# An encoder trunk on one core: transfers behind a power, one activation table for another, squares and gated units moved to later products

## The chip, the cores and the metric

The kernel runs on one core of a Trainium2 chip. The time is the device time of the program in microseconds (us), the median of several runs. The core has a matrix engine (TensorE, PE), a vector engine (VectorE, DVE), an activation engine (ScalarE, ACT), a general engine (GpSimd, POOL) and a queue engine (SyncE, SP) that issues DMAs. ScalarE and GpSimd can issue DMAs as well. Each engine works through its own queue in order; between the queues there are semaphores. TensorE writes its sums to PSUM, of which this kernel uses eight banks in two pools of four ("mm" and "aux").

## What is computed

Two groups of tokens (512 and 256, together T = 768 columns, all widths 1024) go through two layers with shared weights. Cut to what matters here:

```python
def swiglu(h, wg, wu, wd):
    return (jax.nn.silu(h @ wg) * (h @ wu)) @ wd

def even_layer(x, ...):
    x = x + 0.5 * swiglu(rmsnorm(x, f1_n), f1_g, f1_u, f1_d)
    x = x + mixer_ab(rmsnorm(x, mix_n), ...)
    x = x + 0.5 * swiglu(rmsnorm(x, f2_n), f2_g, f2_u, f2_d)
    return x

def odd_layer(x, ...):
    x = x + 0.5 * swiglu(rmsnorm(x, f1_n), f1_g, f1_u, f1_d)
    x = x + mixer_c(rmsnorm(x, mix_n), ...)
    x = x + 0.5 * swiglu(rmsnorm(x, f2_n), f2_g, f2_u, f2_d)
    return x
```

So there are four feed-forward blocks with 2816 hidden columns, and two mixers. Everything is fp32.

## The kernel before

**Precision.** Each fp32 operand is split into a high half (ScalarE rounds it, `whi` for weights, L163) and a low half (VectorE subtracts, `wlo`, L164; for activations L250 and L251). A product is three matmuls per block of 128 rows: high by high, low activation by high weight, high activation by low weight. The low half of the weight is thus needed by the third matmul of a product. The ring of split weights holds five (`NW = 5`).

**Tiling.** The 768 columns lie in two halves of 384, half 0 and half 1. The 2816 hidden columns are taken in 11 pairs of 256. For each pair, gate and up are computed by a Strassen-like scheme of seven products of 2x2 blocks. They are named after the activation operand: b11, b21, t2, t3, t1, b22, n4; each is done for gate and then for up, with 12 matmuls of 384 columns. b11 and b21 use half 0 alone, the others use sums and differences of the halves and of the weight's blocks. Weight sums come partly from DMA: `wsum` (L140) loads one block with SyncE and adds the other to it with an accumulating transfer from GpSimd (L144); other sums are made on VectorE (`sums`, L713).

**Norm.** The scale of the RMS norm is applied after the products. For a half of the columns, ScalarE squares the eight tiles of x and VectorE adds them (`norm_add`, L277); TensorE sums columns into PSUM (`norm_tok`), ScalarE scales (L294), GpSimd takes the power -0.5 (`power`, L314), TensorE turns the result across partitions (`norm_spread`, L198), and ScalarE copies it to `acc` (L455). A gated unit (`hidden`, L579) takes a gate and an up of one half: VectorE multiplies both by `acc` (L585, L587), ScalarE applies Silu (L586), VectorE multiplies them (L588). These feed the operands of the down product: `operands` makes them in eleven steps, six of them splits, five of them differences, and hands them out one at a time to whoever asks.

**Order.** The order of TensorE's instructions is the order in which the code traces them. The other engines' queues are ordered by a planner that follows the traced order where it can; `issue_after(i)` puts instructions of one engine behind instruction `i` in its queue. Two things set what is traced when. `self.after[p, b]` holds functions that run when the up weight of product b in pair p has been split. And `chains` are generators with due times in a clock `self.t` that only counts planned matmul time (1.92 for a product); `run_until` forces them when something needs their result, so that the norm's matmuls are traced there.

**The start.** In the first layer (`behind` is true there) pairs 0, 1 and 2 start with b11 and b21 while the inputs still arrive (`ORDER`, `stages`). Then pair 0 goes on with t2, t3, t1, b22, n4, then pair 1, then pair 2, and the down product of pairs 0 and 1 follows. When the up weight of pair 0's t1 is split, `after[0, "t1"]` runs: eight squares of half 1 and their additions (`squares`), which also starts half 1's norm chain with the delays 9.0 and 3.0, and the gated units of half 0 for pairs 1 and 2. At pair 0's n4, pair 1's transfers and weight sums follow. The gated units of half 1 for pair 0 wait until pair 1's t2 (`later`). The load of an activation table on ScalarE is inserted where an instruction needs a set that is not loaded; the first activation, `first` (L1729), is a Copy.

Of the kernel before, what the change touches and what calls it, by code (L numbers as in the profile page):

```python
# [33 lines left out]
DELAYS = (11.5, 3.0), (9.0, 3.0)  # L34
# [16 lines left out]
class Trunk:  # L51
# [4 lines left out]
    def __init__(self, ctx, tc, aps, phases=PHASES):  # L56
# [8 lines left out]
        self.late = self.mark = self.turn = None  # L65
# [72 lines left out]
    def wsum(self, name, x, y):  # L138

        t = self.fw.tile([P, 4, P], F32, tag="s", name=name, bufs=8)  # L140
        f = t.rearrange("p a b -> p (a b)")
        with self.tc.issue_after(self.late) if self.late else nullcontext():
            self.nc.sync.dma_start(f, x)
        self.nc.gpsimd.dma_start(f, y, accum_op=ALU.add)  # L144
        return t
# [165 lines left out]
    def power(self, y, v):  # L311

        with self.tc.issue_after(self.turn) if self.turn else nullcontext():
            self.nc.gpsimd.tensor_tensor(out=y, in0=v, in1=self.minus[:, : y.shape[1]], op=ALU.pow)  # L314
# [143 lines left out]
    def ffn(self, pre):  # L458
# [50 lines left out]
        def pair(p):  # L509
# [56 lines left out]

            def keep(out, key, n):

                e[n, out] = etile(out)
                nc.scalar.copy(e[n, out], bank[key, n])  # L570
                if p != 1 or out != "u2":
                    next(steps, None)

            def add(key, n, other):
                t = e[n, other]
                nc.vector.tensor_tensor(out=t, in0=bank[key, n], in1=t, op=ALU.add)  # L576
                next(steps, None)
# [17 lines left out]
            def later(f):  # L595
                if p:
                    f()
                else:
                    self.after.setdefault((1, "t2"), []).append(f)
# [39 lines left out]
            def p4():  # L639
                for n in names:  # L640
                    product(n, a[n, 2, 2], "n4", "Y", False)
                    next(steps, None)
                hidden(1, 0, bank["Y", "gate"], bank["Y", "up"])

            def p3():
# [3 lines left out]
                later(lambda: hidden(0, 1, e["gate", "u2"], e["up", "u2"]))  # L649

            if early:
# [6 lines left out]
                yield  # L658
                hidden(0, 0, bank["X", "gate"], bank["X", "up"])
# [7 lines left out]
            if p:  # L667
                load_all()
                if p < EARLY:
                    with self.tc.issue_after(self.behind[1]):  # L670
                        for n in names:
                            sums(n, "s2")
# [13 lines left out]
        units = [lambda: next(stages[1]), lambda: next(stages[2])]  # L686
        if behind:
            self.after[0, "t1"] = [self.squares] + units
        else:
            self.after[0, "t3"] = units  # L690
        self.after[0, "n4"] = [lambda: next(stages[1])]
# [1013 lines left out]
    def build(self):  # L1705
# [20 lines left out]
        elif kind != "last":  # L1726
# [3 lines left out]
            self.np_.tile([P, 6], F32, tag="sm", name="first", bufs=3), self.minus, AF.Copy, scale=1.0  # L1730
# [157 lines left out]
```

## Time and profile before

| | us |
|---|---|
| median of 3 runs | 2585.97 |
| lowest, highest | 2585.16, 2588.82 |
| the profiled run | 2585.71 |
| its span | 2583.9 |

The profile is of one execution. Its page gives busy time by engine; the stage tables give the same for a stretch of time. The waits name the engine and line that waited, what released it, and total, number and longest. A timeline lists start, duration, engine, line, operation and tiles (out<-in), and in square brackets the idle time ahead of an instruction and what ended it. Neighbours of the same kind are merged into one row with their number. Tile names follow the code without buffer numbers; b220h is the high half of block 0 of operand b22.

### The profile page before, as it was taken

Reading aid. Unit: us, or ns where it says so; the run is one execution under the profiler, and the core shown is the slowest. Engines: PE = TensorE matmul, PEld = TensorE weight load, DVE = VectorE, ACT = ScalarE, POOL = GpSimd, SP = SyncE. Lnnn points to the kernel's source line nnn. Section 1 sums busy time; section 2 is a strip of 40 time slices with the busy share of each in tenths; the row PEclk is TensorE's granted clock in tenths of the full one; section 3 lists DMA queues with packets and bytes.
Section 4 is the critical chain, followed back from the end, with each engine's and each line's share of the span. In section 5 each row is a group of like instructions: output and inputs, shape, how many; then the busy total and the mean of one; then the engine's idle time right before and its main releaser. Section 6 shows DMA issues by size and latency. Waiting matters only on the chain.

```text
span 2583.9 us, 42568 instructions
## 1 busy us (share of the span) xinstructions
PE 2557.8 (99%) x15160; PEld 2499.0 (97%) x15160; DVE 2099.9 (81%) x4206; ACT 1370.6 (53%) x2845; POOL 323.3 (13%) x398
## 2 busy tenths in 40 slices
PE   8999999999999999999999999999999999999998
PEld 7999999988899999999999999998999999999998
DVE  8888788879879778788988878886767598878887
ACT  6544454646756545445654445564555475444553
POOL 1111111000111111110111111102212111101100
PEclk9999999999999999999999999999999999999999
DMA  7655556342146545453565455432222256545451
GB/s 205 167 132 126 122 134 159 113 122 68 58 139 158 144 120 130 123 129 88 144 155 135 115 126 127 123 117 77 62 62 65 87 146 168 129 118 124 122 124 51
DMA packets 187156, 310.88 MB, mean 120 GB/s; under 512 B 31680, under 2 KB 46528, under 8 KB 186944
## 3 DMA queue, kind: packets, MB, share of 16 engines
q1 hardware_dynamic: 149792, 240.75, 29.8%
q0 software_dynamic: 36864, 67.13, 16.7%
q8 instruction: 119, 1.95, 0.3%
q14 instruction: 93, 0.76, 0.1%
q10 hardware_dynamic: 288, 0.29, 0.0%
HBM read 298.65 MB, written 15.07 MB: 121 GB/s over the span
## 4 chain that ended last, share of the span: by engine, by line
PE 93%; DVE 3%; ACT 1%; issue 1%; DMA 1%; POOL 0%; ACTq 0%; DVEq 0%; SPq 0%; POOLq 0%
PE ps_mm L187 61%; PE ps_aux L187 31%; PE ps_aux L198 1%; DVE wlo L164 1%; DMA x<-in_x 0%; DVE ol L251 0%; DMA raw<-in_w 0%; DVE s L713 0%; DVE tmp L397 0%; DVE u L576 0%; ACT xh L960 0%; ACT whi L163 0%; POOL sm L314 0%; ACT p L1157 0%; ACT oh L250 0%
## 5 line engine op out<-in xcount | busy, mean ns | idle before, releaser
L163 ACT CAST whi<-s 128x512 fp32r<-128x512 f32 x508 | 310.6, 620 | 404.1 <-PE ps_mm L187 212.7
L164 DVE TENSOR_TENSOR wlo<-s,whi 128x512 fp32r<-128x512 f32 x508 | 344.7, 688 | 180.3 <-ACT whi L163 163.5
L144 POOL DMA_DIRECT2D s<-in_w x256 | 223.6, 914 | 1468.2 <-DVE wlo L164 407.6
L163 ACT CAST whi<-rawp 128x512 fp32r<-128x512 f32 x344 | 211.5, 620 | 265.4 <-PE ps_mm L187 103.1
L164 DVE TENSOR_TENSOR wlo<-rawp,whi 128x512 fp32r<-128x512 f32 x344 | 235.1, 687 | 24.9 <-ACT whi L163 16.6
L187 PE MATMUL ps_mm<-db,whi 128*128 128x384 f32 (+1 forms) x948 | 242.8, 337 | 0.0
L187 PE MATMUL ps_aux<-dt,whi 128*128 128x384 f32 x880 | 225.7, 337 | 0.0
L187 PEld LDWEIGHTS ps_mm<-db,whi 128*128 128x128 f32 x948 | 171.9, 188 | 0.0
L187 PE MATMUL ps_mm<-db,wlo 128*128 128x384 f32 (+1 forms) x474 | 160.0, 337 | 0.6 <-DVE wlo L164 0.6
L187 PEld LDWEIGHTS ps_aux<-dt,whi 128*128 128x128 f32 x880 | 159.8, 188 | 0.0
L187 PE MATMUL ps_aux<-dt,wlo 128*128 128x384 f32 x440 | 148.4, 337 | 0.0
L187 PE MATMUL ps_mm<-xh,whi 128*128 128x512 f32 (+1 forms) x416 | 144.2, 347 | 0.0
L163 ACT CAST whi<-raw 128x512 fp32r<-128x512 f32 x164 | 100.5, 620 | 80.3 <-PE ps_mm L187 55.8
L187 PE MATMUL ps_mm<-xh,wlo 128*128 128x512 f32 (+1 forms) x416 | 140.0, 337 | 0.0
L187 PE MATMUL ps_mm<-xl,whi 128*128 128x512 f32 (+1 forms) x416 | 140.0, 337 | 0.0
L164 DVE TENSOR_TENSOR wlo<-raw,whi 128x512 fp32r<-128x512 f32 x146 | 99.1, 688 | 27.7 <-ACT whi L163 26.5
L576 DVE TENSOR_TENSOR u<-ps_aux,u 128x384 f32<-128x384 f32 x176 | 97.4, 553 | 10.4 <-PE ps_aux L187 8.4
L1157 ACT ACTIVATE p<-p,st 128x256 f32<-128x256 f32 (+3 forms) x144 | 69.0, 481 | 53.4 <-DVE st L1152 53.4
L187 PEld LDWEIGHTS ps_mm<-db,wlo 128*128 128x128 f32 x474 | 88.9, 188 | 1.4 <-DVE wlo L164 1.4
L187 PEld LDWEIGHTS ps_mm<-xh,whi 128*128 128x128 f32 x416 | 78.2, 188 | 10.0 <-issue 1.3
L187 PEld LDWEIGHTS ps_mm<-xh,wlo 128*128 128x128 f32 x416 | 78.1, 188 | 9.4
L187 PEld LDWEIGHTS ps_mm<-xl,whi 128*128 128x128 f32 x416 | 78.3, 188 | 7.5
(508 smaller groups left out, 8059.3 us busy)
## 6 DMA issues: line engine op xcount, KB each, us to landing
rawp<-in_w SPq DMA_DIRECT2D x384, 256.0 KB, 3.2
s<-in_w SPq DMA_DIRECT2D x256, 256.0 KB, 2.9
s<-in_w POOLq DMA_DIRECT2D x256, 256.0 KB, 4.8
raw<-in_w SPq DMA_DIRECT2D x163, 256.0 KB, 2.9
xdm<-x SPq DMA_DIRECT2D x16, 384.0 KB, 2.4
x<-in_x SPq DMA_DIRECT2D x16, 192.0 KB, 4.7
x<-xdm SPq DMA_DIRECT2D x8, 384.0 KB, 3.8
tab<-skew SPq DMA_DIRECT2D x8, 256.0 KB, 4.6
```

Of the source, the lines that this page charges most:

```text
L144: self.nc.gpsimd.dma_start(f, y, accum_op=ALU.add)
L163: i = nc.scalar.copy(hi, src).ins
L164: self.behind = i, (eng or nc.gpsimd).tensor_tensor(out=lo, in0=src, in1=hi.bitcast(F32), op=ALU.subtract).ins
L187: self.nc.tensor.matmul(out, lhsT=lhsT, rhs=rhs, start=start, stop=stop, **kw)
L198: self.nc.tensor.transpose(out, src, self.ident)
L576: nc.vector.tensor_tensor(out=t, in0=bank[key, n], in1=t, op=ALU.add)
L1157: nc.scalar.activation(outs[i - n0], outs[i - n0], AF.Exp, scale=-1.0, bias=mn[:, i : i + 1], accum_out=sm[:, i : i + 1])
```

## The change

It has three parts.

1. In `wsum`, the accumulating transfers of the loads that are marked late (`self.late`: pair 0's sums) are queued on GpSimd behind the last traced power. `power` notes its instruction for this.
2. The first activation of the program uses Silu instead of Copy, so that the table loaded at the start is Silu's.
3. In the first layer, the squares of half 1 run at pair 1's t3, the gated unit of pair 1 at pair 0's n4 (behind pair 1's loads and weight sums), and that of pair 2 at pair 1's t1. Pair 0's units of half 1 run at pair 1's b22 in the first layer and at its t3 in the other three feed-forwards, instead of t2. The delays of half 1's norm become 6.0 and 1.8. The steps of pair 0's operands, which pair 1 asks for, are spread otherwise: in the first layer none at t3, t1 and b22, three at each n4 product and the rest at the end of the pair; in the others two at each addition (t1, b22) and two at each n4.

```diff
-DELAYS = (11.5, 3.0), (9.0, 3.0)
+DELAYS = (11.5, 3.0), (6.0, 1.8)
...
-        self.nc.gpsimd.dma_start(f, y, accum_op=ALU.add)
+        with self.tc.issue_after(self.powered) if self.late and self.powered else nullcontext():
+            self.nc.gpsimd.dma_start(f, y, accum_op=ALU.add)
...
         with self.tc.issue_after(self.turn) if self.turn else nullcontext():
-            self.nc.gpsimd.tensor_tensor(out=y, in0=v, in1=self.minus[:, : y.shape[1]], op=ALU.pow)
+            self.powered = self.nc.gpsimd.tensor_tensor(out=y, in0=v, in1=self.minus[:, : y.shape[1]], op=ALU.pow).ins
...
+            def ahead(n=2):
+                for _ in range(n if p == 1 else 1):
+                    next(steps, None)
+
             def keep(out, key, n):
...
-                if p != 1 or out != "u2":
+                if p != 1:
                     next(steps, None)
 
             def add(key, n, other):
...
-                next(steps, None)
+                ahead(0 if behind else 2)
...
-                    self.after.setdefault((1, "t2"), []).append(f)
+                    self.after.setdefault((1, "b22" if behind else "t3"), []).append(f)
...
                     product(n, a[n, 2, 2], "n4", "Y", False)
-                    next(steps, None)
+                    ahead(3 if behind else 2)
...
+            def second():
+                load_all()
+                if p < EARLY:
+                    with self.tc.issue_after(self.behind[1]):
+                        for n in names:
+                            sums(n, "s2")
...
                 p2()
                 yield
+                if behind and p == 1:
+                    second()
+                    yield
                 hidden(0, 0, bank["X", "gate"], bank["X", "up"])
                 yield
...
             if p:
-                load_all()
-                if p < EARLY:
-                    with self.tc.issue_after(self.behind[1]):
-                        for n in names:
-                            sums(n, "s2")
+                if not (behind and p == 1):
+                    second()
...
         units = [lambda: next(stages[1]), lambda: next(stages[2])]
+        ahead = lambda: next(stages[1])
         if behind:
-            self.after[0, "t1"] = [self.squares] + units
+            self.after[0, "n4"] = [ahead, units[0]]
+            self.after[1, "t3"] = [self.squares]
+            self.after[1, "t1"] = [units[1]]
         else:
             self.after[0, "t3"] = units
-        self.after[0, "n4"] = [lambda: next(stages[1])]
+            self.after[0, "n4"] = [ahead]
...
-            self.np_.tile([P, 6], F32, tag="sm", name="first", bufs=3), self.minus, AF.Copy, scale=1.0
+            self.np_.tile([P, 6], F32, tag="sm", name="first", bufs=3), self.minus, AF.Silu, scale=1.0
```

## Rows read from the trace of the kernel before

**Rows 1.** The page's first part: busy time, share of the span, instructions by engine.
```profile
PE 2557.8 (99%) x15160; PEld 2499.0 (97%) x15160; DVE 2099.9 (81%) x4206; ACT 1370.6 (53%) x2845; POOL 323.3 (13%) x398
```

**Rows 2.** TensorE's waits over the span: for whom, total us, times, longest.
```profile
PE ps_aux L198 <- POOL sm L314: 6.2, 3, 3.3
...
PE ps_mm L187 <- DVE wlo L164: 3.3, 4, 1.3
```

**Rows 3.** Timeline of TensorE, 20 to 31 us: start, duration, instruction, idle ahead.
```profile
20.15 0.80 PE L187 MATMUL ps_aux<-ones,acc 128*128 128x1 f32 x6 [0.17 <-DVE acc L277]
...
26.48 0.59 PE L198 MATMUL ps_aux<-ident,sm 128*128 128x128 f32 x3 [3.30 <-POOL sm L314]
26.78 0.62 PE L187 MATMUL ps_mm<-b211h,whi 128*128 128x384 f32 x1
...
30.07 0.42 PE L187 MATMUL ps_aux<-b110l,whi 128*128 128x384 f32 x1
```

**Rows 4.** Timeline of TensorE, 57 to 91 us.
```profile
57.35 0.69 PE L187 MATMUL ps_aux<-b220h,wlo 128*128 128x384 f32 x1 [5.54 <-DVE wlo L164]
...
60.72 0.46 PE L187 MATMUL ps_aux<-b220h,whi 128*128 128x384 f32 x1
...
62.95 0.72 PE L187 MATMUL ps_aux<-ones,acc 128*128 128x1 f32 x6
...
65.11 0.54 PE L198 MATMUL ps_aux<-ident,sm 128*128 128x128 f32 x3 [0.80 <-POOL sm L314]
...
90.66 0.34 PE L187 MATMUL ps_mm<-t20h,wlo 128*128 128x384 f32 x1
```

**Rows 5.** Stage table: stretch, length, TensorE busy, granted clock, DMA share, GB/s.
```profile
57.30:60.80 3.50, 3.45 (x11) 0.50 0.00 0
```

**Rows 6.** Stage table of VectorE: stretch, length, busy, clock, DMA share, GB/s.
```profile
25.67:89.33 63.66, 56.79 (x110) 0.92 0.60 139
```

**Rows 7.** Timeline of VectorE, 25 to 93 us.
```profile
28.03 0.56 DVE L251 TENSOR_TENSOR t21l<-tmp,t21h 128x384 fp32r<-128x384 f32 x1 [2.36 <-ACT t21h L250]
...
34.64 0.56 DVE L588 SCALAR_TENSOR_TENSOR sg<-sg,v 128x384 f32<-128x384 f32 x1 [2.12 <-ACT sg L586]
...
66.20 0.56 DVE L585 TENSOR_TENSOR u<-u,acc 128x384 f32<-128x384 f32 x1 [1.08 <-ACT acc L455]
...
88.87 0.55 DVE L588 SCALAR_TENSOR_TENSOR u<-u,u 128x384 f32<-128x384 f32 x1
89.33 1.29 DVE L164 TENSOR_TENSOR wlo<-s,whi 128x512 fp32r<-128x512 f32 x2
...
92.07 0.55 DVE L251 TENSOR_TENSOR db<-u,db 128x384 fp32r<-128x384 f32 x1
```

**Rows 8.** Timeline of ScalarE, 22 to 33 us.
```profile
22.07 0.15 ACT L294 ACTIVATE sm<-ps_aux 128x3 f32<-128x3 f32 x1
...
27.11 0.48 ACT L455 COPY acc<-ps_aux 128x384 f32<-128x384 f32 x1 [2.99 <-PE ps_aux L198]
...
32.79 1.28 ACT L586 ACT_TABLE_LOAD   x1
```

**Rows 9.** Timeline of GpSimd, 0 to 130 us.
```profile
21.59 3.74 POOL L144 DMA_DIRECT2D s<-in_w  x4 [18.15 <-DMA s<-in_w]
24.16 2.27 POOL L314 TENSOR_TENSOR sm<-sm,minus 128x3 f32<-128x3 f32 x1
...
63.97 1.09 POOL L314 TENSOR_TENSOR sm<-sm,minus 128x3 f32<-128x3 f32 x1 [19.84 <-ACT sm L294]
```

**Rows 10.** DMA issues of GpSimd at 21.59 and at 24.5: number, size, us to landing.
```profile
s<-in_w POOLq DMA_DIRECT2D x1, 256.0 KB, 5.5
...
s<-in_w POOLq DMA_DIRECT2D x1, 256.0 KB, 10.1
```

**Rows 11.** VectorE's groups by line, 44 to 56 us: busy, mean ns, idle before.
```profile
L277 DVE TENSOR_TENSOR acc<-acc,sq 128x384 f32<-128x384 f32 x7 | 3.8, 546 | 0.0
```

**Rows 12.** Timeline of TensorE, second feed-forward of layer 0.
```profile
808.20 0.45 PE L187 MATMUL ps_mm<-t30h,wlo 128*128 128x384 f32 x1 [1.34 <-DVE wlo L164]
```

More of the change, by code (lines that the diff above doesn't have):

```diff
@@ L64, in __init__ @@
         self.fed_last, self.after = {}, {}
-        self.late = self.mark = self.turn = None
+        self.late = self.mark = self.turn = self.powered = None
         self.first = []
```

## Prediction

> **What bounds the kernel now.** The page's first part comes first: TensorE is busy 99% of the span, so only its idle time and its slow time can be won [rows 1]. The view of its waits then names the idle time: 6.2 us for the power on GpSimd (three times, the longest 3.3) and 3.3 us in four waits for low halves (wlo) of weights [rows 2], beside a longer one shown below. The TensorE timeline puts the large ones into the first layer. One is 3.30 us long and ends at 26.48, where the turned norm of half 0 waits for the power [rows 3]; one is 5.54 us and ends at 57.35, where pair 0's b22 waits for its low half; one is 0.80 us, at 65.11, for half 1's power [rows 4]. After both long waits the matmuls follow each other at about 0.32 us instead of 0.176: from 26.78 to 30.07 ten steps take 3.29 us, 1.53 more than at full rate [rows 3], and from 57.35 to 60.72 eleven take 3.37, 1.44 more [rows 4]; the granted clock there is 0.50, the lower of its two levels, 1.2 of 2.4 GHz [rows 5]. The 0.80 us wait left the matmuls at 0.18. So on TensorE alone 3.30 + 1.53 + 5.54 + 1.44 + 0.80 = 12.6 us lie open.
>
> The second bound shows in the stage table for VectorE: between 25.67 and 89.33 it is busy 56.79 of 63.66 us, idle 6.87 [rows 6]. It ends with the low half for the first product (t2, gate) of pair 2, done at about 90.0 [rows 7] and used by TensorE at 90.66 [rows 4]. All of pairs 0 and 1 stands ahead of it in that queue, so moving work about inside the stretch cannot bring this product forward by more than VectorE's idle time.
>
> **Part by part.**
>
> *Accumulating transfers behind the power.* In the trace the four issues start at 21.59 and hold GpSimd 3.74 us; the power, whose input ScalarE finishes at 22.22 [rows 8], comes behind them and ends at 26.43 [rows 9]. Ahead of them it would start at about 22.3 and take 1.09 us, as the later one does [rows 9], so the turn runs at about 23.45: the wait falls from 3.30 to 0.3, a gain of 3.0, and the 1.5 us of slow matmuls behind it go too. The bounds of the power's own time are 1.09 and the 2.27 us of the first row [rows 9]; I take 1.09, because the longer one overlaps the end of the fourth issue; with 2.27 the gain is 1.9. ScalarE's copy of the scale at 27.11 [rows 8] then comes near 24.2, and VectorE's wait of 2.36 us before 28.03 [rows 7] disappears, since VectorE is busy until 25.67 anyway.
>
> The Trainium skill (GPSIMD Engine Reference, section Specifications) says that GpSimd shares its SBUF interfaces with VectorE and contends with VectorE instructions that read two SBUF inputs, which is what VectorE runs at that moment; by it the power would lie nearer the long end, and the sum above nearer 1.9 than 3.0. The later row of 1.09 us also ran beside such instructions, which speaks against much of it.
>
> The cost is on the transfers: issued 1.86 us later (23.45 instead of 21.59). In the trace the first landed 5.5 us after its issue and the fourth 10.1 after [rows 10], which is 27.1 and about 33.7; moved, the last lands between 33.7 (if the other transfers set the pace) and 35.6. It holds the up weight of t3. VectorE arrives there about 4 us earlier than now, near 34, so its in-order queue can stand 0 to 2 us; I take 0.9. By the Trainium skill (DMA: Bandwidth & Descriptors, section Anatomy of one DMA) a transfer of this size from GpSimd takes about 2.6 us from issue; then nothing would stand here, and the time would be 0.9 lower. The rows of 5.5 and 10.1 disagree with it.
>
> *Silu's table at the beginning.* The load at 32.79 takes 1.28 us [rows 8] and with Silu behind it keeps VectorE waiting 2.12 us before 34.64 [rows 7]. The load at the start exists already (for Copy); it changes its set and not its time. The wait falls to 0 to 0.3. TensorE does not wait there, so this is worth only what VectorE's queue is worth.
>
> *Squares and gated units.* Seven additions of squares (3.8 us busy [rows 11]) and the gated units of pairs 1 and 2 (six VectorE instructions at 0.55, 3.3 us) leave the place ahead of b22's low half: up to 7.1 us for a wait of 5.54, which goes, with the 1.4 us of slow matmuls. Pair 1's unit moves to pair 0's n4 and frees the PSUM banks from which pair 1's t2 starts; three VectorE instructions and a copy into the bank must then fit into n4's second product of 2.1 us; TensorE may wait 0 to 0.9. The squares go behind pair 1's t3, and the gated unit of pair 2 to its t1.
>
> The norm of half 1 moves with the squares. Its delay is 6.0 in the planner's time, while only three products of 1.92 lie between its start and the end of pair 1's t1, where the first gated unit of half 1 asks for the scale. So column sums and turn stand next to each other there, with nothing between. In the trace the sums run from 62.95 for 0.72 and the turn starts at 65.11 [rows 4]; the next matmul could have started near 63.53, so the wait is about 1.6 us where 0.8 stood. VectorE waited 1.08 for the same chain [rows 7], and I leave it 1.0.
>
> On TensorE alone: 12.6 - 0.3 (rest of the first wait) - 1.6 (new wait) = 10.7 us, so pair 2's t2 would be used at 80.0.
>
> On VectorE: of 6.87 us idle, 0.9 (landing), 1.0 (norm chain) and 0.3 (the small ones) remain, so 4.7 go. The slack of 90.66 against 90.0 stays usable for about 0.5: 5.2. Then the order: nine of the eleven steps that split pair 0's units for the down product stand ahead of 89.33 now, and the ninth and eleventh come behind (the first at 92.07 [rows 7]). The change traces six of them at pair 1's n4 and five at its end. If the five again fall behind pair 2's first weights, three steps leave the stretch, each 0.46 in the queue (the distance between the starts at 88.87 and 89.33 [rows 7]): +1.4. That makes 6.6, of which I give 0.2 away for small waits at pair 1's t2. **VectorE sets the gain of the first layer: 6.4 us**, not TensorE's 10.7. What is late next is pair 2's t2.
>
> *The other layers.* Pair 0's second-half units move from pair 1's t2 to its t3. In the second feed-forward of layer 0 TensorE waits 1.34 us before 808.20 for t3's low half [rows 12], which in the code stands behind the six VectorE instructions of those two units; the last feed-forward has its like, since four such waits make 3.3 us and none is over 1.3 [rows 2]. The wait goes, but the steps move as well (two behind each addition), and VectorE is nearly full there too: between 0 and 1.34 each, I take 0.7, together 1.4. The third one has no wait there. Their accumulating transfers already follow the power: 0.
>
> **Sum**: 6.4 + 1.4 = 7.8 us. The profiled run took 2585.71 (span 2583.9, 1.8 around it), 0.26 below the median of 2585.97, against which the time is given: **2578.2 us**.
>
> **Rivals.**
>
> *TensorE's own bound.* If the steps run behind pair 2's first weights (nine at 0.46 are 4.1 us of VectorE work) and the transfers cost nothing (0.9), the queue no longer sets the end: 10.7 + 2.6 = 13.3, 2572.7. For it: the last two steps do slip today. Against: the six at n4 are traced ahead of n4's second weight.
>
> *Strict order.* All eleven steps run before pair 2's weights: 5.2 - 0.9 = 4.3. TensorE then waits over 5 us in one place at pair 2's t2, and the slow matmuls return there (1.5): 2.8, with 0.7 from the other layers 3.5: 2582.5. For it: the squares' additions did stand ahead of b22's low half just as they were traced.
>
> *The power is not earlier*, because something else holds it: VectorE keeps its 2.36 us wait, 2580.6.
>
> *Slower: VectorE stands behind half 1's chain.* The gated units of pair 1 wait for the scale in the middle of VectorE's queue, with the weights of b22 and n4 behind them. Then about 18.4 us of VectorE work remain before pair 2's t2: five gated units of three instructions, eleven steps and four additions at 0.46 (13.8), five low halves and two weight sums at 0.65, half of the pair at 89.33 [rows 7] (4.6). The chain of half 0 took 7.4 us (sums at 20.15 [rows 3], the scale copied at 27.59 [rows 8]); if half 1's takes as long from the end of pair 1's t1 at about 69.5 (the 80.0 above, less four products of 2.1 and 2.2 for the chain itself), with nothing done meanwhile, the weight is ready at 95.3 and used 4.6 later than now; with 1.5 us of slow matmuls and no gain elsewhere, 2592.1. It decides where VectorE starts on that work after 70.8. Against: half 1's chain took 3.2 us in the trace (62.95 to VectorE's next start at 66.20 [rows 4, 7]), and the code lets VectorE run five weights ahead of TensorE.
>
> **How the numbers follow.** Forecast 0.48, TensorE's bound 0.15, strict order 0.25, power not earlier 0.05, slower 0.07. The forecast's own spread is 2575 to 2581 (landing 0 to 2, steps 0 to 1.4, other layers 0 to 2.6). The range reaches to TensorE's bound and past strict order: 2572.5 to 2584. About 0.2% (5.2 us) is what can be told from no change; 2580.8 is the line. Faster: 0.45 of the forecast, 0.15, 0.04 from strict order and 0.03 from the fourth case, 0.67. Slower 0.07. Within: 0.26.
>
> **What would show it.** The power ahead of the four transfers, and TensorE's wait there below 0.5; no table load near 33; no wait at pair 0's b22; sums and turn side by side at the end of pair 1's t1 with 1 to 2 us of wait; VectorE nearly without idle time until pair 2's t2, and TensorE's remaining waits there; no wait at t3 in the second and last feed-forward. It is wrong if VectorE has time to spare while TensorE waits, or if pair 2's t2 starts before 81.

## The result, and the profile after

The changed kernel takes 2591.15 us (median; 2589.22 to 2594.14) where the kernel before takes 2585.97. The ratio is 1.0017 (95% interval 1.0009 to 1.0025): slower by 0.17%, just inside what was called no difference, 13 us above the forecast of 2578.2 and above its range. One of the nine runs of e2 below, the profiled one, took 5630.37 us, so e2's median is that of the other eight and it has no trace to compare.

| | before | after |
|---|---|---|
| median, us | 2585.97 | 2591.15 |
| span of the profiled execution, us | 2583.9 | 2589.3 |
| TensorE busy, us | 2557.8 | 2562.6 |
| VectorE busy, us | 2099.9 | 2099.6 |
| ScalarE instructions | 2845 | 2844 |

The page's first part, for [rows 1]:

```profile
PE 2562.6 (99%) x15160; PEld 2499.3 (97%) x15160; DVE 2099.6 (81%) x4206; ACT 1370.9 (53%) x2844; POOL 325.4 (13%) x398
```

The work is the same but for one table load. TensorE is "busy" 4.8 us longer with as many instructions: part of its time is slower time. Its waits, for [rows 2] (for whom, total us, times, longest):

```profile
PE ps_mm L188 <- DVE wlo L165: 6.7, 9, 2.7
PE ps_aux L199 <- POOL sm L315: 3.5, 3, 1.8
PE ps_aux L188 <- DVE u L581: 3.1, 3, 1.4
PE ps_mm L188 <- ACT whi L164: 2.2, 4, 1.5
```

The power costs 2.7 us less than before. But low halves now cost 6.7 us in nine waits, high halves 2.2, and the third row is new: TensorE waits for VectorE's additions (L581) to free PSUM banks.

**The first stage did what was forecast.** GpSimd, for [rows 9]:

```profile
21.91 0.92 POOL L315 TENSOR_TENSOR sm<-sm,minus 128x3 f32<-128x3 f32 x1 [17.91 <-ACT sm L295]
22.78 3.74 POOL L145 DMA_DIRECT2D s<-in_w  x4
...
69.82 1.09 POOL L315 TENSOR_TENSOR sm<-sm,minus 128x3 f32<-128x3 f32 x1 [2.26 <-ACT sm L295]
```

The power is ahead of the four issues, and TensorE's timeline, for [rows 3] and [rows 4], has no wait at the turn of half 0 and none at pair 0's b22:

```profile
22.88 0.54 PE L199 MATMUL ps_aux<-ident,sm 128*128 128x128 f32 x3
...
70.97 0.54 PE L199 MATMUL ps_aux<-ident,sm 128*128 128x128 f32 x3 [1.44 <-POOL sm L315]
...
81.41 0.44 PE L188 MATMUL ps_mm<-t20h,whi 128*128 128x384 f32 x1 [1.46 <-ACT whi L164]
...
84.77 0.69 PE L188 MATMUL ps_mm<-t20h,wlo 128*128 128x384 f32 x1 [2.74 <-DVE wlo L165]
...
88.14 0.52 PE L188 MATMUL ps_mm<-t20h,whi 128*128 128x384 f32 x1
```

The last rows are pair 2's t2: TensorE was ready for it at 79.95, as worked out (80.0), and used the low half at 84.77, 5.9 us earlier than before. Then ten steps of matmuls take 84.77 to 88.14, 0.34 us each instead of 0.176. The stage table (stretch, length, busy of PE, PEld, DVE, ACT, POOL, clock, DMA share, GB/s):

```profile
84.00:91.00 7.00, 6.23 (x20) 6.23 (x21) 5.86 (x12) 3.60 (x9) 1.83 (x2) 0.51 0.80 180
```

The granted clock there is 0.51, the lower of the two levels. VectorE, for [rows 7]:

```profile
34.17 0.69 DVE L165 TENSOR_TENSOR wlo<-s,whi 128x512 fp32r<-128x512 f32 x1 [0.37 <-ACT whi L164]
...
72.06 0.56 DVE L590 TENSOR_TENSOR u<-u,acc 128x384 f32<-128x384 f32 x1 [1.90 <-ACT acc L456]
...
84.03 0.69 DVE L165 TENSOR_TENSOR wlo<-s,whi 128x512 fp32r<-128x512 f32 x1
```

Between 35 and 84 it stands still once, 1.90 us for half 1's scale; eight of the eleven operand steps stand ahead of the low half at 84.03.

**The later feed-forwards lost.** The same matmul in two traces shows where. The table gives the start of a low-half matmul against the kernel before, in us, at eight places: pair 1's b22 and pair 2's t2 and t3 of the first layer (before: 82.2, 90.7, 94.9), pair 3 of the same feed-forward, behind the first down product (149.6), then t3 in the second feed-forward (808.2), pair 1's b22 in the third (1306.8), pair 3 in the third (1390.7), and the first down product of the fourth, behind its pair 2 (2177.8). Each row is from one execution. The experiments, which the next sections tell, stand below it.

| kernel | 82.2 | 90.7 | 94.9 | 149.6 | 808.2 | 1306.8 | 1390.7 | 2177.8 |
|---|---|---|---|---|---|---|---|---|
| after | -10.5 | -5.9 | -3.0 | -2.7 | -4.2 | -0.1 | +3.7 | +5.2 |
| e3 first layer only | -9.4 | -3.9 | -1.3 | -1.6 | -1.5 | -1.5 | -1.5 | -1.1 |
| e4 power and table only | -3.2 | -3.2 | -3.2 | -2.8 | -2.7 | -2.8 | -2.8 | -2.7 |
| e8 squares and units only | -7.1 | -1.4 | +0.2 | +0.6 | +0.5 | +0.5 | +0.5 | +0.5 |
| e6 steps behind t2 | -9.5 | -8.5 | -8.3 | -1.4 | -1.6 | -1.8 | -1.8 | -1.8 |
| e7 matmuls in the wait | -10.0 | -5.3 | -4.7 | -4.4 | -4.3 | -4.4 | -4.4 | -4.2 |
| e9 last five held | -9.9 | -4.8 | -3.6 | -3.7 | -3.7 | -3.9 | -3.9 | -4.1 |
| e10 squares at t2 | -9.4 | -3.3 | -3.2 | -2.9 | -3.1 | -3.1 | -3.1 | -2.9 |
| e11 t3's low half first | -9.5 | -4.3 | -3.7 | -3.6 | -5.3 | -4.1 | -4.1 | -4.2 |
| e12 less vector work | -9.9 | -4.2 | -4.1 | +1.9 | +0.4 | +3.0 | +3.0 | +1.4 |
| e1 one step per addition | -9.3 | -4.7 | -1.9 | -1.9 | -3.2 | -1.7 | +0.4 | +0.5 |
| e5 steps from t3 | -9.5 | -4.9 | -2.4 | -2.6 | -4.2 | -2.8 | -1.1 | -1.0 |
| e13 changed, with matmuls | -9.4 | -4.8 | -4.2 | -3.9 | -5.4 | -1.9 | +2.5 | +5.2 |

Row "after": 2.7 us are won in the first layer; of 10.5 at pair 1's b22, 4.6 go until pair 2's t2 and 2.9 at the low clock behind it. The t3 wait of [rows 12] is gone (-2.7 to -4.2), but from 149.6 us on the later feed-forwards, with what they win at t3 counted in, lose 2.6, 3.8 and 1.5 (columns 149.6, 1306.8, 1390.7, 2177.8), 7.9 in all: -2.7 + 7.9 = +5.2. In the third one, VectorE's queue in the changed kernel reads:

```profile
1302.83 0.69 DVE L165 TENSOR_TENSOR wlo<-rawp,whi 128x512 fp32r<-128x512 f32 x1 [1.40 <-ACT whi L164]
1303.62 0.56 DVE L252 TENSOR_TENSOR db<-sg,db 128x384 fp32r<-128x384 f32 x1
...
1312.64 0.55 DVE L593 SCALAR_TENSOR_TENSOR u<-u,u 128x384 f32<-128x384 f32 x1
1313.11 0.69 DVE L165 TENSOR_TENSOR wlo<-rawp,whi 128x512 fp32r<-128x512 f32 x1
```

The two low halves are those of n4's gate and up. Between them stand ten operand steps and ten additions and gated-unit instructions, from 1303.62 to 1313.11 with no idle time. TensorE:

```profile
1313.85 0.45 PE L188 MATMUL ps_mm<-n40h,wlo 128*128 128x384 f32 x1 [0.76 <-DVE wlo L165]
...
1330.94 0.44 PE L188 MATMUL ps_aux<-b220h,whi 128*128 128x384 f32 x1 [1.42 <-DVE u L581]
```

The second wait comes from late transfers. GpSimd issued the accumulating transfers for that stretch at 1318.27 and 1319.95, where the kernel before had issued both from 1315.67 on (its row stands second):

```profile
1318.27 0.86 POOL L145 DMA_DIRECT2D s<-in_w  x1 [18.33 <-DVE s L728]
```

```profile
1315.67 1.76 POOL L144 DMA_DIRECT2D s<-in_w  x2 [15.70 <-DVE v L587]
```

VectorE then stood for the sum that the first one brings, ahead of the additions that free the banks; before, it did not (again second):

```profile
1324.97 0.69 DVE L728 TENSOR_TENSOR s<-s,rawp 128x512 f32<-128x512 f32 x1 [1.69 <-issue]
```

```profile
1323.17 0.68 DVE L713 TENSOR_TENSOR s<-s,rawp 128x512 f32<-128x512 f32 x1
```

### The profile page after: what moved, and what is told of

The parts are those of the page before. It is cut to its first block, busy times and chain, and to the rows that moved or that the text cites. A ratio compares the mean times of both kernels' runs of the same rounds, so it can differ in the third digit from the quotient of the medians.

```text
span 2589.3 us, 42560 instructions
## 1 busy us (share of the span) xinstructions
PE 2562.6 (99%) x15160; PEld 2499.3 (97%) x15160; DVE 2099.6 (81%) x4206; ACT 1370.9 (53%) x2844; POOL 325.4 (13%) x398
## 4 chain that ended last, share of the span: by engine, by line
PE 91%; DVE 4%; DMA 2%; issue 2%; ACT 1%; POOL 0%; SPq 0%; ACTq 0%; DVEq 0%; POOLq 0%
PE ps_mm L188 59%; PE ps_aux L188 30%; DMA s<-in_w 1%; PE ps_aux L199 1%; DVE wlo L165 1%; DVE u L581 0%; DVE ol L252 0%; DMA raw<-in_w 0%; DVE s L728 0%; DVE dt L252 0%; DVE db L252 0%; DVE u L593 0%; ACT whi L164 0%; DVE u L592 0%; DMA x<-in_x 0%
## 5 line engine op out<-in xcount | busy, mean ns | idle before, releaser
L581 DVE TENSOR_TENSOR u<-ps_aux,u 128x384 f32<-128x384 f32 x176 | 97.5, 554 | 9.9 <-PE ps_aux L188 8.0
L728 DVE TENSOR_TENSOR s<-s,rawp 128x512 f32<-128x512 f32 x120 | 82.1, 689 | 9.3 <-issue 3.5
```

What stands on the lines that cost most here:

```text
L728: f = lambda o, x, y: self.nc.vector.tensor_tensor(out=o, in0=x, in1=y, op=ALU.add)
```

## Experiments: the later feed-forwards

Two things changed there: pair 0's second-half units went from pair 1's t2 to t3, and the steps were placed differently (none behind the copies of u3, two behind each addition, two behind each n4).

**e1, one step per addition.**

```diff
-                ahead(0 if behind else 2)
+                ahead(0 if behind else 1)
```

> The changed kernel with one operand step instead of two behind each addition in the three later feed-forwards (pair 1's t1 and b22); everything else as changed. Theory A (steps): in the changed kernel's trace these feed-forwards lose 2.4, 4.1 and 1.3 us, because eight steps stand in VectorE's queue ahead of the low half for n4's up product (waits of 0.75 there, then of 1.3 to 1.4 at pair 2's b22), although the wait of 1.34 at t3 went in two of them. With one step per addition those waits go and the 2.6 us at t3 stay won: against the kernel before -2.8 (first layer) - 2.6 = 2580.6 us, ratio 0.9979. Theory B (units): the gated units moved from t2 to t3 cost it, since they fill VectorE just ahead of n4; then it stays at 2589 to 2591, ratio 1.0012 to 1.002.

Measured 1.0003 (0.9994 to 1.0011), 2587.57 us: between the two. The wait at n4 is gone and 3.6 us came back, of the 10.5 expected. The table shows the rest: t3's gain is there (-1.9 to -3.2) and is lost again at pair 2's t2.

**e2, the units back at t2**, steps as changed.

```diff
-    self.after.setdefault((1, "b22" if behind else "t3"), []).append(f)
+    self.after.setdefault((1, "b22" if behind else "t2"), []).append(f)
```

> The changed kernel with pair 0's second-half units of the three later feed-forwards back at pair 1's t2, steps as changed (two behind each addition and each n4). Theory A (steps): the waits at n4-up and at pair 2's b22 stay and the 1.34 us waits at t3 come back in two feed-forwards: 2591.15 + 2.6 = 2593.8, ratio 1.003. Theory B (units): the loss goes with them, the three feed-forwards come back to 0: 2583.2, ratio 0.9989.

Measured 1.0029 (1.0019 to 1.0039), 2594.17 us, as theory A said. Its time is all that there is: whether the waits that theory A names were there is not shown.

**e3, the first layer only**: units at t2 and steps as in the kernel before, in the later feed-forwards.

```diff
-                if p != 1:
+                if p != 1 or not behind and out != "u2":
                     next(steps, None)
...
-                ahead(0 if behind else 2)
+                ahead(0 if behind else 1)
...
-                    self.after.setdefault((1, "b22" if behind else "t3"), []).append(f)
+                    self.after.setdefault((1, "b22" if behind else "t2"), []).append(f)
...
-                    ahead(3 if behind else 2)
+                    ahead(3 if behind else 1)
```

> The first layer as changed, the three later feed-forwards wholly as in the kernel before. By the traces the first layer gains 2.8 to 3.0 us by 130 us and all of the loss is in the other three (2.4 + 4.1 + 1.3 = 7.8): 2585.97 - 2.8 = 2583.2, ratio 0.9989, whichever of the two parts of the later edits is at fault. The rival, that the first layer's own shift sets the later ones back: 2586 or more.

Measured 0.9990 (0.9981 to 0.9999), 2584.16 us, 1.0 above the number expected. From 149.6 us on, its row in the table is flat within 0.5 us: the whole loss lies in the later edits. With e2, the new places of the steps cost 1.0029 - 0.9990 = 0.0039, 10 us. Moving the units to t3 on top of them seems to win 0.0012, 3 us, but the intervals of e2 and of the changed kernel overlap, so this part is not clear of noise.

**e5, steps from t3 on**: the nearest to the old places that the moved units allow.

```diff
+                elif not behind and (out, n) == ("u3", "up"):
+                    ahead(2)
...
-                ahead(0 if behind else 2)
+                ahead(0 if behind else 1)
...
-                    ahead(3 if behind else 2)
+                    ahead(3 if behind else 1)
```

> The changed kernel with the operand steps of the three later feed-forwards as near to the kernel before as the moved units allow: two steps behind t3's second copy again (the first place where all four units of pair 0 exist), then one behind each addition and one behind each n4. Theory A (late start of the steps): in the run with one step per addition VectorE's first step started 1302.04 us, which is 2.0 later against TensorE than in the kernel before, after idle time in which it used to run them, and pair 2's t2 waited for it in each of the three; with the two early steps back the waits go and the 2.6 us won at t3 stay: ratio 0.9979, 2580.6 us where before is 2586. Theory B (the units themselves, at t3, make VectorE late): it stays near the run with one step per addition, ratio 1.0003.

Measured 1.0000 (0.9991 to 1.0008), 2587.01 us: theory B, but by a mechanism that the trace shows to belong to the steps. ScalarE in e5:

```profile
1300.04 0.48 ACT L575 COPY u<-ps_mm 128x384 f32<-128x384 f32 x1
1300.41 0.52 ACT L251 CAST db<-sg 128x384 fp32r<-128x384 f32 x1
```

and VectorE:

```profile
1300.16 0.69 DVE L165 TENSOR_TENSOR wlo<-rawp,whi 128x512 fp32r<-128x512 f32 x1 [1.40 <-ACT whi L164]
1300.95 0.56 DVE L252 TENSOR_TENSOR db<-sg,db 128x384 fp32r<-128x384 f32 x1
```

and the same of the kernel before, ScalarE and VectorE (one product earlier: the copy is that of t3's gate, not of its up, and the low half is b22's, not n4's):

```profile
1300.76 0.47 ACT L570 COPY u<-ps_mm 128x384 f32<-128x384 f32 x1
1301.13 0.52 ACT L250 CAST db<-sg 128x384 fp32r<-128x384 f32 x1
```

```profile
1300.88 0.69 DVE L164 TENSOR_TENSOR wlo<-s,whi 128x512 fp32r<-128x512 f32 x1 [1.40 <-ACT whi L163]
1301.68 0.56 DVE L251 TENSOR_TENSOR db<-sg,db 128x384 fp32r<-128x384 f32 x1
```

Against TensorE, which is 2.8 us earlier in e5 at this point, the step starts 2.1 us later. It needs all four units of pair 0. Behind t3's second weight they exist one product later, and the first half of the step (ScalarE's cast) stands behind a copy that waits for that product. VectorE's low halves are paced by TensorE there (1.40 us of idle time ahead of each), so this is idle time that the steps used before and cannot use now. Behind it VectorE is full up to pair 2's t2, and TensorE waits there:

```profile
1312.51 0.44 PE L188 MATMUL ps_mm<-t20h,whi 128*128 128x384 f32 x1 [0.33 <-ACT whi L164]
...
1313.45 0.44 PE L188 MATMUL ps_mm<-t20h,wlo 128*128 128x384 f32 x1 [0.33 <-DVE wlo L165]
...
1316.09 0.44 PE L188 MATMUL ps_mm<-t20h,wlo 128*128 128x384 f32 x1 [0.29 <-DVE wlo L165]
```

**e11, t3's low half first**: e7 (see the first layer's experiments), and the wait of [rows 12] taken away without moving units or steps.

```diff
-    if early and b in ("b11", "b21") or p == 0 and (b == "t2" or behind and b == "t3"):
+    if early and b in ("b11", "b21") or p == 0 and (b == "t2" or behind and b == "t3") or p == 1 and b == "t3" and not behind:
         stack.enter_context(self.tc.high_priority())
```

> As the run with the 16 idle matmuls, and in the later feed-forwards the low halves of pair 1's t3 ahead of pair 0's second-half units, which stay at t2 (the t3 wait of 1.3 us taken away without moving the units or the steps). If the forecast's mechanism was right (t3's low half stands behind the six instructions of those units) the two waits of 1.3 go, and nothing is added, since the units keep their product and the steps can start where they did: 2.6 us less than the run without, ratio 0.9974, 2579.6. Rival (VectorE is full from there to pair 2's t2, whatever the order): the 1.3 come back at pair 2's t2, ratio 0.9984.

Measured 0.9986 (0.9977 to 0.9995), 2583.21 us, against 0.9984 for e7 without it: the rival. In the second feed-forward, e7 has one wait,

```profile
803.85 0.45 PE L188 MATMUL ps_mm<-t30h,wlo 128*128 128x384 f32 x1 [1.31 <-DVE wlo L165]
```

and e11 has none there, but three at pair 2's t2:

```profile
802.87 0.34 PE L188 MATMUL ps_mm<-t30h,wlo 128*128 128x384 f32 x1
...
819.59 0.44 PE L188 MATMUL ps_mm<-t20h,whi 128*128 128x384 f32 x1 [0.26 <-ACT whi L164]
...
820.58 0.44 PE L188 MATMUL ps_mm<-t20h,wlo 128*128 128x384 f32 x1 [0.36 <-DVE wlo L165]
...
823.19 0.44 PE L188 MATMUL ps_mm<-t20h,wlo 128*128 128x384 f32 x1 [0.26 <-DVE wlo L165]
```

Of the 1.31 us, 0.26 + 0.36 + 0.26 = 0.88 came back as these three waits. By the table 0.5 is left at 1306.8 of the 1.7 that t3 won, and the median is no lower than e7's. So the wait was for the most part no gain: it was slack that TensorE gave VectorE before the stretch in which VectorE is full.

**e12, less vector work**: e11 without the four differences of pair 0's units.

```diff
-            yield sub(h11, h11, h12)
+            yield sub(h11, h11, h12) if q else None
```

(and so for the other three; of the eleven steps the code makes seven splits and four differences, not six and five)

> As the run with t3's low halves first, and the four differences of pair 0's units (four VectorE instructions of 0.47 us in each feed-forward, operand sums of the down product) are left out, so this part of the computation is missing. Nothing else is moved by hand. Theory Q (VectorE's amount of work up to pair 2's t2 sets the end, not its order): 1.9 us less work in each place; the 1.0 and 1.5 us that t3's low halves won and gave back at pair 2's t2 in the second and fourth feed-forward now stay, 2.0 to 2.5, and the first layer gains up to 1.9: ratio 0.9968 to 0.9972, 2578 to 2579. Rival (latency and order, not the amount of work): within 0.5 us of the run without, ratio 0.9985.

Measured 0.9999 (0.9990 to 1.0008), 2587.03 us, against the 0.9968 to 0.9972 expected: a miss, in the first layer. In the second and fourth feed-forward it did as theory Q says: against e11, 1.1 us are kept between t3 and 847 us, and 1.6 between t3 and 2157 us. In the first layer it is level with e11 up to pair 2's t3 (-4.1, -3.7 in the table) and loses behind it. VectorE:

```profile
96.77 0.69 DVE L730 TENSOR_TENSOR s<-s,rawp 128x512 f32<-128x512 f32 x1 [4.53 <-DMA s<-in_w]
```

TensorE:

```profile
103.28 0.45 PE L188 MATMUL ps_aux<-b220h,whi 128*128 128x384 f32 x1 [4.27 <-DVE u L581]
```

and SyncE's queue:

```profile
71.46 13.59 SPq L134 DMA_DIRECT2D rawp<-in_w  x2
85.14 0.86 SPq L143 DMA_DIRECT2D s<-in_w  x2
```

SyncE stood until 85 for a buffer, with the first halves of the sums s queued behind it; in e11 the same pair left at 82.77. GpSimd's accumulating transfers left 2.4 us later than in e11 (88.89 for 86.50) and took longer to land (median 7.9 for 5.0 us). So the sums came late, VectorE stood 4.5 us for them, and the additions that free pair 2's banks were behind it. Leaving out instructions thus moved the transfers too, by a way that is not shown; how much VectorE's work alone is worth in the first layer stays open. (Of the loss by 1306.8, 2.3 us came between 880 and 1200 us, see the last section; the median may include it.)

## Experiments: the first layer

**e4, the power and the table only**, on the kernel before.

```diff
-        self.nc.gpsimd.dma_start(f, y, accum_op=ALU.add)
+        with self.tc.issue_after(self.powered) if self.late and self.powered else nullcontext():
+            self.nc.gpsimd.dma_start(f, y, accum_op=ALU.add)
...
-    self.minus, AF.Copy, scale=1.0
+    self.minus, AF.Silu, scale=1.0
```

> The kernel before with two edits alone: the accumulating transfers behind the power, Silu's table at the start. Theory Q (VectorE's queue sets the end of the first stage): VectorE's waits of 2.36 and 2.12 us go, up to 1 us comes back at the landing of the transfers, the wait of about 5.5 us at pair 0's b22 stays, pair 2's t2 comes 3.5 to 4.5 us earlier: 2581.5 to 2582.5, ratio 0.9983 to 0.9987, as much as the whole change brings in the first layer or more. Theory R (the gain comes only when the squares and the units move too): 2585 to 2586, ratio 1.000.

Measured 0.9988 (0.9979 to 0.9996), 2582.95 us: theory Q, though a little less than it said (pair 2's t2 3.2 us earlier, not 3.5 to 4.5). TensorE's wait is still all there,

```profile
53.80 0.69 PE L188 MATMUL ps_aux<-b220h,wlo 128*128 128x384 f32 x1 [5.54 <-DVE wlo L165]
```

and the row in the table is flat at -3.2 from b22 to pair 2's t2: TensorE's long wait and the slow matmuls behind it cost little there, since VectorE sets the end. It made the low half for pair 2's t2 here:

```profile
86.17 1.29 DVE L165 TENSOR_TENSOR wlo<-s,whi 128x512 fp32r<-128x512 f32 x2
```

The first of the two was done near 86.9 and TensorE used it at 87.50, so without any wait of TensorE some 0.6 us more could have been won at this product. VectorE's idle time tells the gain. It was 6.87 us in [rows 6]; in e4 it is 61.33 - 57.61 = 3.72 in

```profile
25.67:87.00 61.33, 54.41 (x295) 52.60 (x294) 57.61 (x111) 38.24 (x82) 9.19 (x11) 0.94 0.61 148
```

which is 3.15 less, and pair 2's t2 comes 3.2 earlier.

**e8, the squares and units only.** e3 without the two edits of e4.

```diff
-        with self.tc.issue_after(self.powered) if self.late and self.powered else nullcontext():
-            self.nc.gpsimd.dma_start(f, y, accum_op=ALU.add)
+        self.nc.gpsimd.dma_start(f, y, accum_op=ALU.add)
...
-self.minus, AF.Silu, scale=1.0
+self.minus, AF.Copy, scale=1.0
```

> In the first layer only the third part of the change: squares and gated units spread over pair 1's products, the power behind the four accumulating transfers and Silu's table late as before; later feed-forwards as before. Theory Q (VectorE's queue sets the end): pair 0's b22 wait of 5.5 us goes, but pair 2's t2 is no earlier than VectorE's queue lets it, which keeps its waits of 2.36 and 2.12 us: gain 0 to 1.5, ratio 0.9995 to 1.000, and worse by up to 2.5 if the clock falls behind pair 2's t2. Theory P (TensorE's own waits set the end): the 5.54 and the 1.44 us of slow matmuls go, 1.6 comes at the norm of half 1: gain 5, ratio 0.998.

Measured 1.0004 (0.9995 to 1.0013), 2588.66 us: theory Q with the clock. The table has -7.1 at pair 1's b22, -1.4 at pair 2's t2 and +0.2 at its t3; the granted clock between 89 and 93 is 0.57. So TensorE's long wait can go without bringing pair 2's t2 much forward: the first two edits win what the first layer wins; the third, by itself, nothing.

**e6, the steps behind t2.** e3 with all eleven steps held back until behind pair 2's t2.

```diff
-                    ahead(3 if behind else 1)
+                    ahead(0 if behind else 1)
...
+                if behind and p == 2:
+                    for _ in self.held:
+                        pass
...
```

> The later feed-forwards as before; in the first layer all eleven operand steps of pair 0 stand behind pair 2's t2 instead of six at pair 1's n4 and five at its end. Theory F (strict order): seven steps of 0.47 us stood ahead of pair 2's t2 low half, so it comes about 3.3 us earlier, the waits of 1.5 and 2.7 there shrink to under 1.0, the matmuls behind stay at 0.18 us: 5.5 to 7 us less than with the steps where the change put them, 2577 to 2579, ratio 0.9967 to 0.9973. Theory G (backlog): VectorE stays the bound until about 100 us, and TensorE waits for the same work a product or two later: 2581 to 2584, ratio 0.998 to 0.999.

Measured 0.9995 (0.9986 to 1.0004), 2585.07 us: theory G, and a little worse. Pair 2's t2 comes at 82.2, by the table 4.6 us earlier than in e3 and 2.6 earlier than in the changed kernel (theory F: about 3.3), with no slow matmuls. Then b22 of the same pair:

```profile
98.96 0.69 PE L188 MATMUL ps_aux<-b220h,whi 128*128 128x384 f32 x1 [4.17 <-DVE u L581]
```

VectorE has not stood still for longer than 0.23 us since 84; the additions that free the banks wait behind the eleven steps. The wait has only moved, and the slow matmuls with it: the granted clock between 99 and 104 is 0.50, and the table goes from -8.3 to -1.4.

**e7, matmuls in the wait.** e3, with matmuls whose result nobody reads, ahead of pair 2's t2.

```diff
             def p6():
+                if behind and p == 2:
+                    self.warm(16)
```

> First layer as changed, later feed-forwards as before, and 16 matmuls of 128x512 whose result nobody reads, put ahead of pair 2's t2, where TensorE otherwise waits about 1.2 and 2.7 us. They change no other engine's work. Theory C (clock): the loss between pair 2's t2 and t3 (from -4.1 to -1.8 us in the run without them) comes from the granted clock after the waits; with TensorE kept busy it stays at 1.0 and 2.0 to 2.5 us come back: ratio 0.9981, 2581.5. Theory D (those matmuls are slow for another reason, such as operands that come late): no change, ratio 0.999.

Measured 0.9984 (0.9975 to 0.9993), 2582.24 us, as theory C said. The intervals of e3 and e7 overlap, so the traces decide. e7:

```profile
80.35 3.84 PE L195 MATMUL ps_aux<-onesr 128*128 128x512 f32 x16
84.02 0.33 PE L188 MATMUL ps_mm<-t20h,whi 128*128 128x384 f32 x1
85.33 0.45 PE L188 MATMUL ps_mm<-t20h,wlo 128*128 128x384 f32 x1 [0.80 <-DVE wlo L165]
```

Its stage table:

```profile
85.50:90.50 5.00, 4.78 (x26) 4.37 (x27) 5.00 (x11) 3.29 (x8) 1.82 (x2) 1.00 0.57 125
```

and that of e3:

```profile
87.00:92.00 5.00, 5.00 (x17) 5.00 (x16) 3.86 (x9) 2.54 (x6) 1.69 (x2) 0.50 0.70 140
```

TensorE works off 26 instructions instead of 17 in 5 us, VectorE is no longer held up by it (busy 5.00 of 5 us, for 3.86), and from pair 2's t2 to its t3 e7 gives 0.6 us away, e3 2.6. These 2.0 us are what the clock is worth; the medians differ by 1.9. (At t3 the rows differ by 3.4, but 1.4 of that stood at t2 already, from slow matmuls behind half 1's turn in e3's execution, see the last section.)

**e13, the changed kernel with the same matmuls** (the diff of e7, on the changed kernel).

> The changed kernel, and 16 matmuls of 128x512 whose result nobody reads ahead of the first layer's pair 2 t2. Theory C (clock): the matmuls of pair 2's t2 follow at 0.18 instead of 0.32 us and 2 to 2.9 us come back: ratio 1.0017 - 0.0009 = 1.0008 (1.0006 to 1.0009), about 2588.5. Rival: no change, ratio 1.0017.

Measured 1.0012 (1.0003 to 1.0021), 2589.19 us: 0.0005 less, about half of the 0.0009 that was expected. Its stage table against the changed kernel's 20 matmuls at 0.51:

```profile
84.00:91.00 7.00, 5.95 (x31) 5.12 (x31) 7.00 (x15) 5.29 (x13) 1.82 (x2) 1.00 0.78 195
```

From pair 2's t2 to its t3 it gives 0.6 us away, the changed kernel 2.9; at 149.6 us the table has -3.9 for -2.7. In the profiled execution this gain is not kept: it took 2591.31 us, one of e13's slowest, and ends at +5.2 like the changed kernel. So the clock as the cause of the slow matmuls is shown by two traces; the medians of two pairs of runs point the same way, but neither difference alone is outside its interval.

**e9 and e10** asked for more on top of e7. e9 holds the last five steps behind pair 2's t2:

```diff
-            for _ in steps:
+            for _ in steps if not behind or p != 1 else ():
...
+            if behind and p == 1:
+                self.held = steps
...
```

> First layer as changed with the 16 idle matmuls ahead of pair 2's t2, later feed-forwards as before, and in the first layer the last five operand steps of pair 0 held back until behind pair 2's t2 (the first six stay at n4). Theory Q (VectorE's queue is full until about 100 us, so work moved behind one product is paid at a later one): within 1 us of the run with the matmuls, ratio 0.998 to 0.9988. Theory O (only the order ahead of pair 2's t2 counts): pair 2's t2 comes 1 to 2 us earlier and stays so, ratio 0.9976 or less.

Measured 0.9983 (0.9974 to 0.9992), 2582.34 us: theory Q. e10 puts the squares behind pair 1's t2:

```diff
-            self.after[1, "t3"] = [self.squares]
+            self.after[1, "t2"] = [self.squares]
```

> As the run with the 16 idle matmuls, and the squares of half 1 behind pair 1's t2 instead of t3, one product pair earlier. VectorE stood about 1.9 us (70.2 to 72.1 in the changed kernel) for the scale of half 1, with all of the gated units behind it. Theory Q (VectorE's idle time is what counts there): the scale comes earlier, those 1.9 us go, pair 2's t2 comes up to 1.9 earlier: ratio 0.9977 to 0.998, about 2580.5. Rival: the additions then stand ahead of the low halves of t3 and t1, which TensorE uses first, and a wait of 1 to 3 us takes its place there: 0.9985 to 0.9995.

Measured 0.9985 (0.9976 to 0.9994), 2582.64 us: nothing won. VectorE's wait for the scale shrank as said,

```profile
71.03 1.03 DVE L590 TENSOR_TENSOR u<-u,acc 128x384 f32<-128x384 f32 x2 [0.39 <-ACT acc L456]
```

but pair 2's t2 came at 87.4, 2.0 later than in e7: eleven steps stand ahead of its low half in this queue, eight in e7's. Three steps of 0.47 are 1.4 us of it; the rest stays open. The rival's wait came too, though shorter than it said: TensorE waited 0.66 us at 58.43 (t2) and 0.66 at 79.94 (n4).

Of all these, e7 has the lowest median, 2582.24 us, under both kernels; e9, e10, e4 and e11 lie within 1 us of it, less than their intervals tell apart.

## Why the prediction was wrong, step by step

**The power ahead of the transfers: right.** The turn ran at 22.88 without a wait (0.3 was kept back for one), and the clock did not fall behind it. The power took 0.92 us, below both bounds (1.09 and 2.27). The longer end, which the Trainium skill's rule on shared interfaces (GPSIMD Engine Reference, Specifications) was weighed for, is not supported by this row: VectorE formed a low half from two inputs (wlo<-raw,whi, from 21.99 for 0.68 us) beside it.

**Landing: smaller.** 0.9 us was taken, VectorE lost 0.37. The two issues recorded between 22.5 and 24 us landed after

```profile
s<-in_w POOLq DMA_DIRECT2D x2, 256.0 KB, 6.6
```

so the 0.9 came out smaller for another reason than a short transfer: 6.6 us is far from the 2.6 that the forecast estimated from the fit on the Trainium skill's page (DMA: Bandwidth & Descriptors, Anatomy of one DMA). The four left 1.19 us later than before (22.78 for 21.59), not 1.86, since the power was short.

**Silu's table: right.** One ScalarE instruction less, and VectorE's 2.12 us [rows 7] are gone.

**Half 1's norm: sizes off.** TensorE waits 1.44 (1.6 forecast), VectorE 1.90 (1.0).

**TensorE's own sum: one step miscounted, without consequence.** From 57.35 to 60.72 there are eleven matmuls but ten steps, so the slow time there is 1.61 us more, not 1.44, and TensorE's total 12.8, not 12.6. TensorE's sum did not set the gain.

**VectorE's bound: the mechanism right, the number partly luck.** Pair 2's t2 was to come 6.4 earlier and came 5.9 earlier; e4 repeats the argument with other terms (3.15 us less idle, 3.2 earlier). Inside it, VectorE's idle time fell by 4.5 (6.87 to 2.41; 4.7 forecast), where the shorter landing (0.37 for 0.9) and the longer norm chain (1.90 for 1.0) happened to cancel. The step "three steps leave the stretch" failed: two stood behind pair 2's first weight before and three do now, so one left, and the work in the stretch fell by 0.84 us instead of 1.4.

**Where the 13 us lie.** The first layer was to win 6.4 and kept 2.7 (3.7 short, by the table at 149.6); the other layers were to win 1.4 and lost 7.9 (9.3 short).

**The clock behind the wait: the term left out.** The forecast had TensorE ready at 80.0 and the low half used at 84.3: over 4 us of waiting at pair 2's t2, from its own numbers. It put slow matmuls there only into the rival "strict order", at 1.5 us. They came, and cost 2.9 (e7 and e13 show that it is the clock). The first layer's gain is 3.0 at pair 2's t3 instead of 6.4, about what that rival said (2.8), by another road: eight steps ahead, not eleven.

**The other layers: the sign was wrong.** Forecast +1.4 us, measured -7.9. The step that failed is "the wait goes, but the steps move as well ... I take 0.7". The wait did go (1.3 us each time, in after, e1, e5 and e11), but in e1, e5 and e11 most of it came back at pair 2's t2, and in e12 it stayed won, where work was left out. The steps, bounded there at a loss of the same 1.3, cost 10 us (e2 against e3). In the changed kernel's trace ten of them stand ahead of n4's second low half, and the transfers and additions of pair 2 come late behind them; that the same rows make up e2's 10 us is likely but not shown, since e2 has no trace. "The third one has no wait there", and so nothing to lose, was the worst of it: it lost 3.8. The bound looked at the wait that the change takes away, not at the slack that the moved steps would eat further on.

**Rivals.** TensorE's bound did not come, and e6, which made pair 2's t2 the least late, shows why: VectorE's work is paid two products later. The slower rival named the right place and wrong sizes: VectorE did stand for half 1's scale and went on from 72.06, but the chain took 3.2 us (from 68.81), not 7.4, and the work from there to pair 2's low half 12.0 us (to 84.03) instead of the 18.4 that it counted, because the low halves of b22 and n4 had been made ahead of it (57.7 to 69.5).

## What to carry to other kernels

A wait ahead of a stretch in which another engine is full is that engine's slack. Before counting it as a gain, follow the busy engine's queue to the next place where it has idle time, and ask what is late there. And where a forecast leaves TensorE waiting several microseconds in one place, the slow matmuls behind that wait belong into the sum; a few idle matmuls in the wait were worth some 0.05% here, by medians whose intervals overlap.

Moving work that others depend on (the units) moves all that depends on it (eleven steps, their casts on an in-order engine, the buffers and transfers behind them), by a whole product even if it moves by one line.

## What the runs showed of the hardware that was not expected

A wait of 1.30 to 1.53 us for the power of half 1 is in eleven traces with the moved squares. In five of them (e3, e8, e9, e11, e12) the matmuls behind it ran at 0.32 us (in e3 from 72.04 to 75.07, granted clock 0.50), in the other six (the changed kernel, e1, e5, e6, e7, e13) at 0.18. So at this length of wait the clock fell in some executions and not in others, and a gain that hangs on it differs from run to run.

In e12, 2.3 us were lost between 880 and 1200 us against e11, spread smoothly: between 880 and 1000 us TensorE worked off 682 matmuls in e12 and 688 in e11, with no waits and a granted clock of 1.00 in both. Nothing in the profile names a cause. Differences of this size between two traces are therefore no evidence without a wait or a clock that goes with them; the comparisons above that are smaller rest on such rows.
